# A mixture-of-experts transformer block: the first eight experts' results added to rows in DRAM by DMAs, the others scattered by matmuls as before, and activations turned in 32x32 blocks on VectorE

## The chip, the cores and the metric

The kernel runs on one core of one Trainium2 chip. The metric is the time of one execution on the device in microseconds (us); the median of three runs stands for the kernel. The profile is of one further execution of the same program. The engines are called by their short names: PE multiplies matrices (PEld is its loading of the stationary operand), DVE is VectorE, ACT is ScalarE, POOL is GpSimd, SP is SyncE, which here does nothing but issue DMAs.

## What is computed

One layer of a diffusion transformer over 512 tokens of width 1024: token mixing by latent attention and Fourier groups, then a mixture of experts that takes most of the time. Everything is float32. The part that matters here, cut from the reference:

```
logits = h @ w_router + b_router;  top_logit, top_idx = top_k(logits, 4)      # h: 512 x 1024, 32 experts
gates = softmax(top_logit)
per expert e, for the tokens that chose it:
    g = min(xb @ w_gate[e] + b_gate[e], 7);  u = clip(xb @ w_up[e] + b_up[e], -7, 7)
    y = (g * sigmoid(1.702 * g) * (u + 1)) @ w_down[e] + b_down[e]
    out[token] += gate * y
x + g2 * rms_norm(out, norm_ffn_post)
```

Each expert has three matrices of 1024 x 1024, 4.19 MB each. All 32 experts are read once, 402.7 MB together.

## The kernel before

The first quarter of the span is attention, Fourier mixing and the router. The rest is a chain of 32 **units**, one for each expert. A unit's **kind** says how many token slots it has: h 128, m 96, l 64, t 32. Units 0 and 1 are experts 0 and 1 (kind m). The other thirty experts are ranked by their number of tokens on the chip and fill fifteen **pairs**, one large unit and one small: units 2 and 3 are (m, t), 4 and 5 (m, l), 6 and 7 (m, l), 8 and 9 (h, t), and so on. In all there are 4 h, 13 m, 10 l and 5 t. An expert that has more tokens than its unit has slots is left to a loop after the end.

A unit has three **steps**, g, u and d, for its three matrices, written (4,g) and so on. `order` is written by hand: (0,g) (0,u) (1,g) (0,d) (1,u) (2,g) (1,d), and then, pair by pair, (3,g) (2,u) (3,u) (2,d) (3,d) (4,g) (5,g) (4,u) ... A step is eight chunks of 128 rows of its matrix. `step_mm` (L1538) multiplies one chunk: for an m unit twelve products of 32 stationary columns by 256 moving ones, in four column groups of PE that work side by side; for an l unit two products of 64 by 512; for a t unit four of 32 by 256; for an h unit six of 128 by 512 in the faster format float32r, high and low part of each operand apart. The profile counts a float32 product as two matmul instructions.

The weights come in **pieces** of two chunks (1 MB), issued by SP (`load_piece`, L965 to L978) into a ring of eleven slots. SP issues the next piece only when PE has done with the piece that held the slot. The queues of every engine run in the order in which the program is written; nothing is reordered.

Between its chunks a step does side work, one or two items a chunk (`side_step`): the tokens' rows are fetched from DRAM by an indirect DMA (`gather`, on POOL), turned by PE (`x_trans`), and after step u the activations are turned too. **`a_trans`** (L1441) does that in all kinds: PE transposes of 128 x 128 into PSUM (eight for h, six for m, four for l, two for t), copied to SBUF by ACT. `glu_g` and `glu_u` form the activations on DVE and ACT.

After step d the result must go to its tokens. **`y_out`** (L1475) copies it from PSUM, times the gate, as a high and a low part in float32r (ACT and DVE). `back` makes on DVE a table of ones that says which slot belongs to which token, and **`scatter`** (L1512) multiplies it with the result on PE: for each of four blocks of 128 tokens and two halves of 512 columns two products for an m or h unit and one for an l or t unit; DVE adds each sum to `acc`, four tiles of 128 x 1024 in SBUF. Unit 0 and unit 1 are scattered alone; from unit 2 on a pair is scattered together. The scatter of unit 0 has a third product that adds the gated `b_down` biases of all experts. After the last unit `acc` is normed and written out.

Of the kernel before, what the change touches and what calls it, by code (L numbers as in the profile page):

```python
# [36 lines left out]
D = 1024  # L37
# [125 lines left out]
def dit_block(ctx: ExitStack, tc: tile.TileContext, x, c, cctx, c_ctx, w_mod, b_mod, n_ap, n_ao, n_fp, n_fo,  # L163
# [6 lines left out]
    hx2_d = dr.tile([SEQ, D], F32, name="hx2_d")  # L170
    x1_d = dr.tile([SEQ, D], F32, name="x1_d")
    vec_d = dr.tile([4, D], F32, name="vec_d")

    NRING = 11
    NX = 5
# [1 line left out]
    WT = 1  # L177
    WN = {2: 4, 3: 4, 4: 4, 5: 4}
    NB, LA = 4, 3
    EARLY = (1, 2, 3)  # L180
    LATER = (0, 1, 1, 1, 1, 1, 1, 1)
    V = nc.vector
# [1068 lines left out]
        nc.gpsimd.memset(z.f, 0.0)  # L1251

    SLOTS = {"h": 128, "m": 128, "l": 64, "t": 32}

    def onehot_slots(kind, p_):
        n = SLOTS[kind]
# [32 lines left out]
    def gather(u, kind):  # L1289

        b = tbank()
        for t in range(4):
            mm(ps[:, b, 0:4], S1.r[:, t], R3[kind].r[:, t], start=t == 0, stop=t == 3)

        def fetch():
            cp(iv.f, ps[:, b, 0:4])
            stt(iv.f[:, 0:1], iv.f[:, 1:2], CRp("negT_" + ("h" if kind == "m" else kind)), iv.f[:, 0:1], op0=OP.mult, op1=OP.add)
            if u:
                tt(idxs.i[:, u:u + 1], iv.f[:, 0:1], CRp("addT_" + ("h" if kind == "m" else kind)), op=OP.add)
# [140 lines left out]

    def a_trans(kind):  # L1441
        a = glu_tiles(kind)[1]
        for half in range(2 if kind in "hm" else 1):
            b = tbank()
            n = min(4, WIDTH[kind] // 128 - 4 * half)
            for k in range(n):
                c = (4 * half + k) * 128
                tr(ps[:, b, k * 128:k * 128 + 128], a[:, c:c + 128])
            src = ps[:, b, 0:n * 128].rearrange("p (k n) -> p k n", k=n)
            c4 = slice(4 * half, 4 * half + 4)  # L1450
            if kind == "h":
                split_late(aTh.r[:, c4], aTl.r[:, c4], src)
            else:
                z = (aTm if kind == "m" else aTf.f)[:, 4 * half:4 * half + n]
                later(lambda src=src, z=z: act(z, src, AF.Copy), [z], [src], age=0)
            yield

    def glu_g(kind, b):
        t_, u_ = glu_tiles(kind)
# [8 lines left out]
    def glu_u(kind, b, wait=1):  # L1468
        t_, u_ = glu_tiles(kind)
        ts(u_, sums(kind, b), LIMIT, -LIMIT, op0=OP.min, op1=OP.max)  # L1470
        stt(u_, u_, 1.0, t_, op0=OP.add, op1=OP.mult)
        for _ in range(wait):
            yield

    def y_out(u, kind, b):  # L1475
        g = gcol.f[:, u:u + 1]
# [35 lines left out]
    def scatter(*us):  # L1512

        for t in range(4):
            for h in range(2):
                b = tbank()
                c, tk = slice(512 * h, 512 * h + 512), slice(128 * t, 128 * t + 128)
                terms = []
                for u in us:
                    if kinds[u] in "hm":  # L1520
                        rw = slice(0, 128 if kinds[u] == "h" else 96)
                        terms += [(ST["h"].r[rw, tk], z.r[rw, c]) for z in (yh, yl)]
                    else:
                        terms.append(small_term(kinds[u], tk, h))
                if us == (0,):
                    terms.append((gT.r[0:96, tk], bd.r[0:96, c]))
# [3 lines left out]
                if us == (0,):  # L1530
                    later(lambda z=z, b=b: cp(z, ps[:, b]), [z], [ps[:, b]], age=0)
                else:
                    later(lambda z=z, b=b: tt(z, z, ps[:, b], op=OP.add), [z], [z, ps[:, b]], age=0)
            yield

    MAT = {"g": 0, "u": 1}
# [1 line left out]
    def step_mm(kind, mat, b, k, w, hi, lo, sel, xs):  # L1538

        first = k == 0  # L1540
        if kind == "h":
# [6 lines left out]
            for st, mv, last in ((xh, hi, False), (xh, lo, False), (xl, hi, k == 7)):  # L1548
                for h in range(2):
                    mm(ps[:, b + h], st.r[:, k], mv.r[:, h * 512:h * 512 + 512], start=first, stop=last)  # L1550
                first = False
        elif kind == "m":
# [8 lines left out]
            both = ps[96:128, b].rearrange("p (r n) -> p r n", r=2)  # L1561
            if first:
                bias = biasP.b[0:96, MAT.get(mat, 0)]
                if mat != "d":
                    for p in range(3):
                        mm(out_(0, p, 2), sel.to_broadcast([96, 32]), bias[:, 0:512], start=True, stop=False)
                else:
                    sel = selb.b[0:96, NS + 2:NS + 3]
                mm(both, sel.to_broadcast([96, 32]), bias[:, None, 768:D].to_broadcast([96, 2, 256]), start=True,
                   stop=False)  # L1570
                if mat != "d":
                    for p in range(4):
                        q = unit(2, p)[1]
                        mm(out_(2, p), sel.to_broadcast([96, 32]), bias[:, q * 256:q * 256 + 256], start=True, stop=False)
            for r in range(3):
                for p in range(4):
                    g, q = unit(r, p)
                    n = 1
                    if mat != "d":
                        st = xs[:, k, 32 * g:32 * g + 32]  # L1580
                    else:
                        fq, c = k // 2, k % 2
                        st = xs[:, 2 * fq + c, 32 * g:32 * g + 32] if fq < 3 else xs[:, 2 * g + c, 96:128]
                        if first and p < 3 and r < 2:
                            if r:
                                continue
                            n = 2
                    mm(out_(r, p, n), st, w[:, q * 256:q * 256 + 256 * n],
                       start=first and mat == "d" and (p < 3 or r == 2), stop=k == 7 and r > 0)
        else:  # L1590
            v, n = (64, 512) if kind == "l" else (32, 256)
            a, c = k // (n // 128), k % (n // 128)
            st = xs[:, c, v * a:v * a + v]
            if first and mat != "d":
                for h in range(128 // v):
                    mm(ps[v * h:v * h + v, b, 0:n], sel.to_broadcast([96, v]),
                       biasP.b[0:96, MAT[mat], h * n:h * n + n], start=True, stop=False)
                first = False
            for h in range(128 // v):
                mm(ps[v * h:v * h + v, b, 0:n], st, w[:, h * n:h * n + n], start=first, stop=k == 7)  # L1600

    def sel_of(u):
        kind, e, r = units[u]
# [69 lines left out]
    for i, (u, m) in enumerate(order):  # L1673
        kind = kinds[u]
        if i:
# [2 lines left out]
            if was == "g":  # L1678
                add(glu_g(pk, pb), True)
            elif was == "u":  # L1680
                acted[pu] = add(chain(glu_u(pk, pb, {"h": 2, "m": 2, "l": 3, "t": 5}[kind]), a_trans(pk)), True)
            else:
                finish(summed)
                y_out(pu, pk, pb)
                if pu == 1:
                    summed = add(chain(chain_back(pu), scatter(pu)))
                elif pk in "lt":
                    summed = add(chain(chain_back(pu - 1), chain_back(pu), scatter(pu - 1, pu)))
        if i == 5:
            summed = add(chain(bdown(), chain_back(0), scatter(0)))  # L1690
        if i == 1:
            ready[1] = add(x_of(1))
        elif i == 2:
# [27 lines left out]
        elif i == 1:  # L1721
# [5 lines left out]
            aTm = alias(aTh, 6, 128)  # L1727
            yh, yl = R(D), R(D)
            acc = [W(D) for _ in range(4)]

            bdr = acc[3]
# [7 lines left out]
        elif i == 6:  # L1739
# [1 line left out]
                finish(side.pop(0))  # L1741
            settle()
            free(bd, g3, gT)
            aTf, u1l, yz = W(4, 128), W(512), R(D)

    while side:
        finish(side.pop(0))
# [136 lines left out]
```

## Time and profile before

| | |
|---|---|
| median of three runs | 1416.8 us (1412.1 to 1417.2) |
| the profiled execution's own time | 1413.2 us |
| its span, first to last instruction | 1411.4 us |
| PE busy | 1345.5 us, 95% of the span |
| DVE, ACT, POOL busy | 719.9, 409.3, 121.8 us |
| bytes moved by DMA | 468.9 MB, mean 332 GB/s |

The share of busy time of PE must be read with care: the ends of matmuls are modelled, and a busy engine may still be paced by something else. The rate of the DMAs in a stretch, and the time from one PE group's start to the next one's, say more. The expert part begins at about 338 us and its last product ends at about 1388 us.

### The profile page before, as it was taken

Reading aid. Unit: us, or ns where it says so; the run is one execution under the profiler, and the core shown is the slowest. Engines: PE = TensorE matmul, PEld = TensorE weight load, DVE = VectorE, ACT = ScalarE, POOL = GpSimd, SP = SyncE. Lnnn points to the kernel's source line nnn. Section 1 sums busy time; section 2 is a strip of 40 time slices with the busy share of each in tenths; the row PEclk is TensorE's granted clock in tenths of the full one; section 3 lists DMA queues with packets and bytes.
Section 4 is the critical chain, followed back from the end, with each engine's and each line's share of the span. In section 5 each row is a group of like instructions: output and inputs, shape, how many; then the busy total and the mean of one; then the engine's idle time right before and its main releaser. Section 6 shows DMA issues by size and latency. Waiting matters only on the chain. (4 is left out here: it accounts for less than half of the span.)

```text
span 1411.4 us, 30490 instructions
## 1 busy us (share of the span) xinstructions
PE 1345.5 (95%) x12966; PEld 798.2 (57%) x12967; DVE 719.9 (51%) x1329; ACT 409.3 (29%) x634; POOL 121.8 (9%) x90
## 2 busy tenths in 40 slices
PE   5998999998999999999999999999999999999993
PEld 3766887877554545466444454654544466444572
DVE  4676777755452424268423335762324287232575
ACT  5565455632110101035110103421111154010352
POOL 4355000013000000000000000000000000000002
PEclk8999999999998999999999999999999999999997
DMA  9865003667887999999999999999999999999993
GB/s 343 306 229 189 1 0 106 216 228 313 315 295 298 408 397 408 379 409 392 405 409 379 409 374 409 396 408 406 393 384 385 401 395 408 402 408 375 408 380 122
DMA packets 126496, 468.86 MB, mean 332 GB/s; under 512 B 10976, under 2 KB 12316, under 8 KB 126356
## 3 DMA queue, kind: packets, MB, share of 16 engines
q1 hardware_dynamic: 121540, 454.44, 83.2%
q0 software_dynamic: 4816, 12.43, 2.3%
q8 instruction: 103, 1.69, 0.5%
q14 instruction: 37, 0.30, 0.1%
HBM read 464.05 MB, written 6.31 MB: 333 GB/s over the span
## 5 line engine op out<-in xcount | busy, mean ns | idle before, releaser
L266 PE MATMUL ps<-s,s 128*32 128x256 f32 (+11 forms) x5364 | 892.4, 417 | 28.7 <-DMA s<-in_w_mod_dram 8.4
L266 PEld LDWEIGHTS ps<-s,s 128*128 128x128 f32 (+4 forms) x5033 | 510.8, 155 | 315.2 <-issue 182.2
L266 PE MATMUL ps<-s,a 128*32 128x256 f32 (+1 forms) x7026 | 412.7, 383 | 0.0
L266 PEld LDWEIGHTS ps<-s,a 128*32 128x32 f32 x7026 | 216.7, 110 | 158.5 <-issue 18.9
L274 ACT ACTIVATE s<-s 128x1024 fp32r<-128x1024 f32 (+8 forms) x196 | 175.9, 927 | 361.7 <-DVE s L283 308.4
L278 DVE TENSOR_TENSOR s<-s,s 128x1024 fp32r<-128x1024 f32 (+11 forms) x316 | 208.4, 686 | 32.3 <-ACT s L274 28.6
L274 ACT ACTIVATE s<-ps 128x512 fp32r<-128x512 f32 (+5 forms) x168 | 91.3, 553 | 246.0 <-PE ps L266 127.1
L278 DVE TENSOR_TENSOR s<-s,ps 128x512 f32<-128x512 f32 (+1 forms) x129 | 86.5, 682 | 82.1 <-PE ps L266 81.7
L285 DVE TENSOR_SCALAR s<-ps 128x768 f32<-128x768 f32 (+3 forms) x32 | 26.3, 823 | 185.1 <-PE ps L266 185.1
L270 PE MATMUL ps<-s,s 128*128 128x128 f32 x575 | 96.6, 288 | 15.3 <-DVE s L283 9.9
L1302 POOL DMA_INDIRECT s<-hx_d,s x31 | 32.4, 1045 | 893.3 <-PE ps L266 613.2
L270 PEld LDWEIGHTS ps<-s,s 128*128 128x128 f32 x575 | 66.4, 143 | 73.7 <-issue 45.8
L293 DVE COPY s<-ps 128x4 f32<-128x4 f32 (+5 forms) x66 | 23.7, 359 | 141.0 <-PE ps L266 117.0
L274 ACT ACTIVATE a<-ps 128x512 f32<-128x512 f32 (+1 forms) x48 | 25.9, 540 | 219.0 <-PE ps L270 219.0
L278 POOL TENSOR_TENSOR s<-s,s 128x1024 f32<-128x1024 f32 (+1 forms) x23 | 53.7, 2339 | 272.9 <-DVE s L278 211.4
L289 DVE SCALAR_TENSOR_TENSOR s<-ps,s,s 32x256 fp32r<-32x256 f32 (+5 forms) x64 | 46.2, 721 | 58.0 <-ACT s L274 52.0
L274 ACT ACTIVATE s<-ps,s 32x256 fp32r<-32x256 f32 (+7 forms) x68 | 44.8, 669 | 97.9 <-PE ps L266 90.5
L297 DVE TENSOR_TENSOR s<-ps,s 128x512 fp32r<-128x512 f32 (+1 forms) x92 | 60.6, 667 | 22.9 <-ACT s L274 22.8
L283 DVE TENSOR_SCALAR s<-ps 128x768 f32<-128x768 f32 (+4 forms) x33 | 26.5, 803 | 77.6 <-PE ps L266 77.5
L274 ACT ACTIVATE s<-s,s 128x1 f32<-128x1 f32 (+4 forms) x70 | 43.2, 644 | 13.8 <-DVE s L289 7.7
L297 DVE TENSOR_TENSOR s<-s,s 128x192 fp32r<-128x192 f32 (+5 forms) x32 | 36.0, 1144 | 8.5 <-ACT s L274 8.5
L289 DVE SCALAR_TENSOR_TENSOR s<-s,s,s 128x512 fp32r<-128x512 f32 (+5 forms) x48 | 36.8, 796 | 5.9 <-ACT s L274 4.6
(77 smaller groups left out, 289.4 us busy)
## 6 DMA issues: line engine op xcount, KB each, us to landing
s<-in_w_gate_dram SPq DMA_DIRECT2D x128, 1024.0 KB, 10.9
s<-in_w_up_dram SPq DMA_DIRECT2D x128, 1024.0 KB, 10.8
s<-in_w_down_dram SPq DMA_DIRECT2D x128, 1024.0 KB, 7.9
s<-in_w_mod_dram SPq DMA_DIRECT2D x32, 512.0 KB, 4.6
s<-in_w_mod_dram SPq DMA_DIRECT2D x8, 1024.0 KB, 16.3
s<-in_x_dram SPq DMA_DIRECT2D x8, 512.0 KB, 8.3
s<-in_w_out_dram SPq DMA_DIRECT2D x8, 512.0 KB, 5.1
s<-in_w_in_dram SPq DMA_DIRECT2D x1, 2560.0 KB
```

The costliest lines, as they stand in the source:

```text
L266: pin(nc.tensor.matmul(o, a, b, start=start, stop=stop))
L270: pin(nc.tensor.transpose(o, i, ident))
L274: return nc.scalar.activation(o, i, f, **kw)
L278: return eng.tensor_tensor(o, a, b, op=op)
L283: eng.tensor_scalar(o, a, s1, s2, op0=op0)
L285: eng.tensor_scalar(o, a, s1, s2, op0=op0, op1=op1)
L289: V.scalar_tensor_tensor(o, a, s, b, op0=op0, op1=op1)
L293: eng.tensor_copy(o, i)
L297: later(lambda: eng.tensor_tensor(lo, src, hi, op=OP.subtract), [lo], [src, hi])
L1302: nc.gpsimd.indirect_dma_start(out=xg[kind], out_offset=None, in_=src, in_offset=bass.IndirectOffsetOnAxis(ap=idxs.i[:, u:u + 1], axis=0), ...
```

## The change

It has two parts.

**Adding in DRAM.** For units 0 to 7 (`NADD = 8`) there is no `y_out`, no `back` and no `scatter`. `y_rows` copies the result times its gate from PSUM to one SBUF tile (`yd`, or `yd2` for l and t) in plain float32, and `y_send` has POOL issue one indirect DMA that adds its rows to those of `acc_d` in DRAM; unused slots point outside and are skipped. Before the first of them `first_rows` forms the bias product, copies it to `acc` on ACT and writes the four tiles to `acc_d` (2 MB). After unit 7's rows are sent, POOL issues four DMAs that read `acc_d` back into `acc` (2 MB), and units 8 to 31 are scattered by PE as before.

**Turning on VectorE.** For m, l and t units steps g and u are laid out anew: the stationary operand is 32 tokens, and the four column groups of PE take four interleaved sets of columns, each of eight runs of 32 columns of the chunk (`cols`). An m unit still has twelve products a chunk, a t unit four; an l unit has eight of 32 by 256 in place of two of 64 by 512. With that layout `a_trans` is one DVE transpose of 32 x 32 blocks for each 32 tokens, from SBUF to SBUF (three for m, two for l, one for t), without PE, PSUM or ACT. Units of kind h are unchanged.

```diff
@@ a_trans @@
+        if kind == "h":
...
+            return
+        for s in range(ROWS[kind] // 32):
+            o = (aTm if kind == "m" else aTf.f)[:, :, 32 * s:32 * s + 32]
+            i_ = a[:, 256 * s:256 * s + 256].rearrange("p (b r) -> p b r", r=32)
+            guard([o], [i_])
+            V.transpose(o, i_)
+        yield
@@ new @@
+    def y_rows(u, kind, b):
+        g = gcol.f[:, u:u + 1]
...
+            for s in range(3):
+                rw, cl = slice(32 * s, 32 * s + 32), slice(256 * s, 256 * s + 256)
+                cp(yd[rw, c3], y[96:128, cl])
+            act(yd[0:96, 0:768], y[0:96], AF.Copy, scale=g[0:96])
+            ts(yd[0:96, c3], yd[0:96, c3], g[0:96], None, op0=OP.mult)
+        else:
+            act(yd2[:, 0:WIDTH[kind]], ps[:, b, 0:WIDTH[kind]], AF.Copy, scale=g)
+    def y_send(u):
...
+        nc.gpsimd.indirect_dma_start(out=acc_d if nt == 1 else acc_d.rearrange("t (c n) -> (t c) n", c=nt),
+                                     out_offset=bass.IndirectOffsetOnAxis(ap=idxs.i[rw, u:u + 1], axis=0), in_=src,
+                                     in_offset=None, bounds_check=nt * SEQ - 1, oob_is_err=False, compute_op=OP.add)
+    def first_rows():
+        for t in range(4):
+            for h in range(2):
+                b = tbank()
+                c, tk = slice(512 * h, 512 * h + 512), slice(128 * t, 128 * t + 128)
+                mm(ps[:, b], gT.r[0:96, tk], bd.r[0:96, c], start=True, stop=True)
+                act(acc[t].f[:, c], ps[:, b], AF.Copy)
+            nc.gpsimd.dma_start(acc_d[128 * t:128 * t + 128], acc[t].f)
+            yield
+        y_send(0)
@@ step_mm, steps g and u of m, l and t @@
+            def cols(z, q):
+                return z.rearrange("p (b q r) -> p q b r", q=4, r=32)[:, q]
...
+            for s in range(n):
+                for q in range(4):
+                    mm(tile_(q, s), x_cols(32 * s), cols(w, q), start=False,
+                       stop=k == 7 and (s % 2 == 1 or s + 1 == n))
@@ after a step d @@
-                y_out(pu, pk, pb)
-                if pu == 1:
-                    summed = add(chain(chain_back(pu), scatter(pu)))
-                elif pk in "lt":
+                if pu < NADD:
+                    y_rows(pu, pk, pb)
+                    if pu:
+                        y_send(pu)
+                    if pu + 1 == NADD:
+                        for t in range(4):
+                            nc.gpsimd.dma_start(acc[t].f, acc_d[128 * t:128 * t + 128])
+                else:
+                    y_out(pu, pk, pb)
+                if pk in "lt" and pu >= NADD:
                     summed = add(chain(chain_back(pu - 1), chain_back(pu), scatter(pu - 1, pu)))
         if i == 5:
-            summed = add(chain(bdown(), chain_back(0), scatter(0)))
+            summed = add(chain(bdown(), first_rows()))
```

The first place where the order on an engine changes is PE's step (3,g), a t unit, in which unit 1 was scattered. Before, its rows begin like this (`s_3463` is the t unit's x, `s_3015` and `s_3016` are the high and low part of unit 1's result, `s_2719` the table of ones):

```order
L266 MATMUL ps<-s_2537,s_3463 32x256 x8
L266 MATMUL ps<-s_3015,s_2719 128x512
L266 MATMUL ps<-s_3016,s_2719 128x512
L266 MATMUL ps<-s_3015,s_2719 128x512
L266 MATMUL ps<-s_3016,s_2719 128x512
L266 MATMUL ps<-s_2545,s_3463 32x256 x4
```

With the change the same step on PE reads as follows (`s_3459` is the t unit's x); it goes from its bias products straight through its chunks:

```order
L268 LDWEIGHTS s_2598
L268 MATMUL ps<-s_1973,s_2598 32x256
L268 MATMUL ps<-s_2538,s_3459 32x256 x8
L268 MATMUL ps<-s_2546,s_3459 32x256 x8
L268 MATMUL ps<-s_2554,s_3459 32x256 x8
L268 MATMUL ps<-s_2562,s_3459 32x256 x8
```

No product of the scatter is left in that step. The second place is POOL's queue from the fetch of unit 4 on, which before held fetches alone (`hx_d` are the tokens' rows, `s_2733` and `s_2734` the buffers of large and of small units):

```order
L1302 DMA s_2733<-hx_d,s_2729 128x1024
L1302 DMA s_2734<-hx_d,s_2729 128x512
```

With the change the same stretch of POOL's queue holds the writes of `acc_d` and the adding DMAs between the fetches (`a_3018` is `yd`, `a_3731` is `yd2`):

```order
L1305 DMA s_2734<-hx_d,s_2730 128x1024
L1514 DMA acc_d<-s_3019 128x1024
L1514 DMA acc_d<-s_3020 128x1024
L1514 DMA acc_d<-s_3021 128x1024
L1514 DMA acc_d<-s_3022 128x1024
L1502 DMA acc_d<-a_3018,s_2730 512x1024
L1305 DMA s_2735<-hx_d,s_2730 128x512
L1502 DMA acc_d<-a_3018,s_2730 512x1024
```

The first adding DMA follows the four writes, and the fetch of unit 5 stands behind it in the queue.

## Rows read from the trace of the kernel before

**Rows 1.** The page: busy time of PE, then the DMAs' rate in 40 slices.

```profile
PE 1345.5 (95%) x12966; PEld 798.2 (57%) x12967; DVE 719.9 (51%) x1329; ACT 409.3 (29%) x634; POOL 121.8 (9%) x90
...
GB/s 343 306 229 189 1 0 106 216 228 313 315 295 298 408 397 408 379 409 392 405 409 379 409 374 409 396 408 406 393 384 385 401 395 408 402 408 375 408 380 122
```

**Rows 2.** Windows: from:to, us, busy (count) by engine, PEclk, DMA share, GB/s.

```profile
410.00:460.00 50.00, 47.13 (x603) 25.61 (x605) 18.75 (x36) 3.59 (x7) 1.00 (x1) 0.86 0.74 274
460.00:1372.00 912.00, 902.82 (x9204) 473.65 (x9193) 412.45 (x749) 204.95 (x291) 27.29 (x26) 1.00 1.01 398
480.00:490.00 10.00, 8.09 (x110) 4.56 (x114) 5.57 (x18) 1.86 (x4) 1.00 (x1) 1.00 1.03 408
```

**Rows 3.** Waits: of SP's queue in the whole span, of PE from 460 to 1380.

```profile
SPq L978 <- PE ps L266: 728.5, 323, 21.3
...
PE ps L266 <- DVE s L278: 6.8, 8, 1.8
```

**Rows 4.** Timeline of PE in step (1,g): start, us, what, count.

```profile
366.50 0.66 PE L270 MATMUL ps<-s,s 128*128 128x128 f32 x4
367.08 1.50 PE L266 MATMUL ps<-s,s 128*32 128x256 f32 x24
368.52 0.44 PE L270 MATMUL ps<-s,s 128*128 128x128 f32 x2
368.89 6.06 PE L266 MATMUL ps<-s,s 128*32 128x256 f32 x100
```

**Rows 5.** Timeline of PE: scatter of unit 0 in (2,g), then step (3,g).

```profile
406.55 1.68 PE L266 MATMUL ps<-s,s 96*128 96x512 f32 x6
...
430.30 1.16 PE L266 MATMUL ps<-s,s 96*32 96x256 bf16 x20
434.33 13.73 PE L266 MATMUL ps<-s,s 96*128 96x512 f32 x72 [2.87 <-DVE s L283]
447.88 4.49 PE L266 MATMUL ps<-s,a 128*32 128x256 f32 x80
```

**Rows 6.** Timeline of PE: one of four groups, scatters of (2,3) and (4,5).

```profile
487.73 2.23 PE L266 MATMUL ps<-s,s 96*128 96x512 f32 x6 [0.41 <-DVE s L283]
...
556.16 1.67 PE L266 MATMUL ps<-s,s 96*128 96x512 f32 x6
```

**Rows 7.** The page: software queue (packets, MB, share), DMA issues.

```profile
q0 software_dynamic: 4816, 12.43, 2.3%
...
x_d<-s POOLq DMA_DIRECT2D x4, 512.0 KB, 3.7
hx_d<-s POOLq DMA_DIRECT2D x4, 512.0 KB, 6.1
...
s<-hx_d,s POOLq DMA_INDIRECT x31, 6.8
```

**Rows 8.** Groups by shape, DVE, 440 to 1380 us.

```profile
L283 DVE TENSOR_SCALAR s<-ps 128x768 f32<-128x768 f32 x10 | 9.6, 958 | 20.7 <-PE ps L266 20.7
L289 DVE SCALAR_TENSOR_TENSOR s<-s,s 128x256 f32<-128x256 f32 x5 | 2.1, 424 | 0.2
```

**Rows 9.** Timeline of PE: value products in attention; half of an l unit's step u.

```profile
210.50 1.67 PE L266 MATMUL ps<-s,s 128*128 128x256 f32 x12
...
521.41 3.84 PE L266 MATMUL ps<-s,s 96*64 96x512 bf16 x18
```

**Rows 10.** The end: SP's load after the weights, a window, ACT's copy of unit 31.

```profile
1372.91 0.35 SPq L1754 DMA_DIRECT2D s<-vec_d  x1
...
1370.00:1375.00 5.00, 5.00 (x24) 3.93 (x23) 4.97 (x7) 4.40 (x6) 0.00 (x0) 1.00 0.92 353
...
1383.38 1.92 ACT L274 ACTIVATE s<-ps,s 32x256 fp32r<-32x256 f32 x4 [0.99 <-PE ps L266]
```

**Rows 11.** Windows around the scatter of unit 1, columns as in the second group.

```profile
430.00:440.00 10.00, 7.13 (x56) 3.35 (x44) 4.86 (x8) 2.05 (x4) 0.14 (x1) 0.68 0.75 301
440.00:450.00 10.00, 10.00 (x92) 5.02 (x92) 3.72 (x7) 0.42 (x1) 0.00 (x0) 0.64 0.52 182
```

More of the change, by code (lines that the diff above doesn't have):

```diff
@@ L172, in dit_block @@
     vec_d = dr.tile([4, D], F32, name="vec_d")
+    acc_d = dr.tile([SEQ, D], F32, name="acc_d")
     NRING = 11
@@ L179, in dit_block @@
     NB, LA = 4, 3
+    NADD = 8
     EARLY = (1, 2, 3)
@@ L1297, in fetch @@
             stt(iv.f[:, 0:1], iv.f[:, 1:2], CRp("negT_" + ("h" if kind == "m" else kind)), iv.f[:, 0:1], op0=OP.mult, op1=OP.add)
+            tt(idxs.i[:, u:u + 1], iv.f[:, 0:1], CRp("addT_" + ("h" if kind == "m" else kind)), op=OP.add)
             if u:
-                tt(idxs.i[:, u:u + 1], iv.f[:, 0:1], CRp("addT_" + ("h" if kind == "m" else kind)), op=OP.add)
                 nt = 128 // SLOTS[kind]
@@ L1442, in a_trans @@
         a = glu_tiles(kind)[1]
[L1443 to L1451, printed above, removed]
-                split_late(aTh.r[:, c4], aTl.r[:, c4], src)
[L1453 to L1456, printed above, removed]
+        if kind == "h":
+            for half in range(2):
+                b = tbank()
+                for k in range(4):
+                    c = (4 * half + k) * 128
+                    tr(ps[:, b, k * 128:k * 128 + 128], a[:, c:c + 128])
+                src = ps[:, b].rearrange("p (k n) -> p k n", k=4)
+                c4 = slice(4 * half, 4 * half + 4)
+                split_late(aTh.r[:, c4], aTl.r[:, c4], src)
+                yield
[6 more added lines that the diff above has]
+        yield
     def glu_g(kind, b):
@@ L1473, in glu_u @@
             yield
+    def y_rows(u, kind, b):
+        g = gcol.f[:, u:u + 1]
+        if kind == "h":
+            act(yd, flat2(b, D), AF.Copy, scale=g)
+        elif kind == "m":
+            y, c3 = flat2(b, 768), slice(768, D)
+            for s in range(3):
[6 more added lines that the diff above has]
+    def y_send(u):
+        kind = kinds[u]
+        nt, rw = 128 // SLOTS[kind], slice(0, 96 if kind == "m" else 128)
+        src = yd[rw] if kind in "hm" else yd2[:, 0:WIDTH[kind]]
+        guard([], [src, idxs.i[:, u:u + 1]])
+        nc.gpsimd.indirect_dma_start(out=acc_d if nt == 1 else acc_d.rearrange("t (c n) -> (t c) n", c=nt),
[4 more added lines that the diff above has]
+            for h in range(2):
+                b = tbank()
+                c, tk = slice(512 * h, 512 * h + 512), slice(128 * t, 128 * t + 128)
+                mm(ps[:, b], gT.r[0:96, tk], bd.r[0:96, c], start=True, stop=True)
+                act(acc[t].f[:, c], ps[:, b], AF.Copy)
+            nc.gpsimd.dma_start(acc_d[128 * t:128 * t + 128], acc[t].f)
+            yield
+        y_send(0)
     def y_out(u, kind, b):
@@ L1529, in scatter @@
                 z = acc[t].f[:, c]
[L1530 to L1533, printed above, removed]
+                later(lambda z=z, b=b: tt(z, z, ps[:, b], op=OP.add), [z], [z, ps[:, b]], age=0)
             yield
@@ L1551, in step_mm, with x_cols, tile_ @@
                 first = False
+        elif mat != "d":
+            n = ROWS[kind] // 32
+            def x_cols(o):
+                m, v = {"m": (8, 0), "l": (4, 64), "t": (2, 32)}[kind]
+                return xs[:, k % m, v * (k // m) + o:v * (k // m) + o + 32]
+            def cols(z, q):
+                return z.rearrange("p (b q r) -> p q b r", q=4, r=32)[:, q]
+            def tile_(q, s, n=1):
+                return ps[32 * q:32 * q + 32, b + s // 2, 256 * (s % 2):256 * (s % 2) + 256 * n]
+            if first:
+                for s in range(0, n, 2):
+                    m = min(2, n - s)
+                    for q in range(4):
+                        z = cols(biasP.b[0:96, MAT[mat]], q)
+                        o = tile_(q, s, m)
+                        if m == 2:
+                            o = o.rearrange("p (m b r) -> p m b r", m=2, r=32)
+                            z = z[:, None].to_broadcast([96, 2, 8, 32])
+                        mm(o, sel.to_broadcast([96, 32]), z, start=True, stop=False)
+            for s in range(n):
+                for q in range(4):
+                    mm(tile_(q, s), x_cols(32 * s), cols(w, q), start=False,
+                       stop=k == 7 and (s % 2 == 1 or s + 1 == n))
         elif kind == "m":
@@ L1558, in out_ @@
                 return ps[32 * p:32 * p + 32, b + r // 2, 256 * (r % 2):256 * (r % 2) + 256 * n]
-            both = ps[96:128, b].rearrange("p (r n) -> p r n", r=2)
             if first:
[L1563 to L1574, printed above, removed]
+                both = ps[96:128, b].rearrange("p (r n) -> p r n", r=2)
+                zero = selb.b[0:96, NS + 2:NS + 3].to_broadcast([96, 32])
+                mm(both, zero, biasP.b[0:96, 0][:, None, 768:D].to_broadcast([96, 2, 256]), start=True, stop=False)
             for r in range(3):
@@ L1578, in step_mm @@
                     n = 1
[L1579 to L1589, printed above, removed]
+                    if first and p < 3 and r < 2:
+                        if r:
+                            continue
+                        n = 2
+                    mm(out_(r, p, n), xs[:, k, 32 * g:32 * g + 32], w[:, q * 256:q * 256 + 256 * n],
+                       start=first and (p < 3 or r == 2), stop=k == 7 and r > 0)
         else:
             v, n = (64, 512) if kind == "l" else (32, 256)
[L1592 to L1598, printed above, removed]
             for h in range(128 // v):
-                mm(ps[v * h:v * h + v, b, 0:n], st, w[:, h * n:h * n + n], start=first, stop=k == 7)
+                mm(ps[v * h:v * h + v, b, 0:n], xs[:, k, 0:v], w[:, h * n:h * n + n], start=first, stop=k == 7)
     def sel_of(u):
@@ L1726, in dit_block @@
             aTh, aTl = R(8, 128), R(8, 128)
-            aTm = alias(aTh, 6, 128)
+            aTm = alias(aTh, 8, 96)
             yh, yl = R(D), R(D)
+            yd = alias(yh, D)
             acc = [W(D) for _ in range(4)]
@@ L1743, in dit_block @@
             free(bd, g3, gT)
-            aTf, u1l, yz = W(4, 128), W(512), R(D)
+            aTf, u1l, yz = W(8, 64), W(512), R(D)
+            yd2 = alias(yz, 512)
     while side:
```

5 lines of the change are left out of this document (2 added, 3 removed).

## The prediction

> **What bounds the kernel now.** I read the page first: PE is busy 95% of the span, and from slice 14 to slice 39 the DMAs move 374 to 409 GB/s [rows 1]. Both look full, so the question is which of them paces the other. The windows tell: where the DMAs are undisturbed they move 408 GB/s, also while POOL fetches rows; but from 460 to 1372 us they average 398, and from 410 to 460 only 274 [rows 2]. The list of waits says why. SP waits 728.5 us in all for PE to give a ring slot back, while in the expert part PE's longest entry is 6.8 us in total for DVE, and no DMA stands in its list at all [rows 3]. So **PE sets the pace**, by a small margin: the weights could come only some percent faster. The kernel has two limits close together, and a change must be counted against both.
>
> **PE's account.** Turning goes off PE. In an m unit four transposes stand from 366.50 to 367.08 us and two from 368.52 to 368.89 [rows 4]: 0.58 + 0.37 = 0.95 us. An l unit has four (0.58), a t unit two (0.37). For 13 m, 10 l and 5 t that is 12.4 + 5.8 + 1.9 = 20.0 us.
>
> The scatters of units 0 to 7 go too. Unit 0's are four groups of 1.68 us [rows 5], of which a third, the bias product, stays: 4 x 1.68 x 2/3 = 4.5 us. Unit 1's lie in step (3,g), which takes from 430.30 to 447.88 us, 17.6 us [rows 5]. Its own work is 64 instructions; 80 of that size take 4.49 us, so 3.6 us are its own and 14.0 us go: PE first stands 2.87 us for DVE's table of ones, and then runs at half its clock, 1.2 GHz, for a while (mean 0.68 and 0.64 in two windows [rows 11]). Units 2 and 3 have four groups of 2.23 us, 8.9 us; units 4 and 5 four of 1.67, 6.7 us, and 6 and 7 the same [rows 6]. Together 40.8 us.
>
> The new layout of steps g and u costs PE nothing if a strided moving operand is read as fast as a plain one. For an l unit a chunk becomes sixteen instructions of 4.49/80 = 0.056 us, 0.90 us; now eighteen instructions (four chunks and the bias) take 3.84 us, 0.9 a chunk [rows 9]. The count for m and t stays.
>
> So PE alone would end 20.0 + 40.8 = 60.8 us sooner. Against the profiled execution's own 1413.2 us (span 1411.4) that is **1352 us**, if the weights were always there.
>
> **The DMAs' account.** They are not. From 410 us on the stream carries 50 x 274 + 912 x 398 kB = 376.7 MB up to 1372 us [rows 2]. At 408 GB/s that takes 923.2 of the 962 us: 38.8 us of slack, no more, whatever PE saves. I start at 410 because there the ring is full and PE is at the first scatter; before it PE loses only unit 0's transposes, 1 us.
>
> The change also adds bytes, on the same DMAs. `acc_d` is written once and read once: 2 x 2.10 MB. The adds carry the same rows as the fetches. POOL's queue moved 12.43 MB, of which the eight DMAs of x_d and hx_d are 4.19 [rows 7]; the rest over 31 fetches is 0.266 MB each, so eight adds hold 2.13 MB. No row shows an adding DMA. Below I price it like a fetch (factor 1); above like four fetches. I take 2, since it must read the old row as well as the new one. That gives 4.19 + 4.25 = 8.44 MB or 20.7 us; 15.5 us at factor 1, 31.1 at 4. The Trainium skill (Collectives: The Full Stack, The bandwidth ceiling) says that an add in the DMA path needs two source reads for one write; by that the price is again twice a copy's. No run here shows it.
>
> The stream thus saves 38.8 - 20.7 = **18.1 us** (7.7 to 23.3).
>
> **The end and the beginning.** The last weights land at about 1373.7 us (353 GB/s in 1370 to 1375, with vec_d's 0.5 MB in it), and ACT copies the last unit's result at 1383.4 [rows 10]. PE lags 9.7 us behind the stream now, since it is the slower one; paced by the stream it lags one piece of a t unit, 0.9 us. That is 0 to 8.8 us; I take 6, because in the (m, l) pairs PE stays about as slow as the stream. With 1 us from the start: 1413.2 - 18.1 - 6 - 1 = **1388 us**. Since 1388 lies above 1352, the DMAs are the bound and two thirds of PE's saving turns into waits for weights.
>
> **What hides the rest.** DVE's transposes take about 0.42 us per 256 columns (its nearest rows, 424 and 958 ns for 256 and 768 [rows 8]); three and the two operations before them are 3.2 us, behind the small unit's step u of 7 us (l) or 3.6 us (t). With twice the price it is 4.5 us, which only the single (m, t) pair would feel. If that cover were gone, 28 units would pay up to 3 us each. The adds bring one new wait: `yd` is filled again for unit 1 when unit 0's add has landed. That add waits for the four writes of `acc_d` (3.7 to 6.1 us to land [rows 7]) and itself needs about 6.8. DVE and ACT may stand some 5 us there, behind them unit 2's activations; PE has steps (3,g) and (2,u), about 14 us, before it asks for those. On POOL the fetch of unit 5 stands behind that add and is needed two steps later still. Both cost nothing. What becomes late in place of PE is the weights: PE should wait for them first in (2,d) to (5,u), when the ring has run empty.
>
> **The rivals.** *Strided reads* (slower). If PE reads runs of 32 columns 128 apart more slowly, steps g and u pay: 16 chunks x (13 x 1.34 + 10 x 0.90 + 5 x 0.45) = 459 us of work. From 8% PE is the bound again (1352 + 37 = 1389), from 13% nothing is gained, at 20% it is 1352 + 92 = 1444 us. The nearest row speaks against it: the value products of attention read two runs of 128 columns 256 apart, twelve in 1.67 us, 0.14 us for 256 columns with the loading [rows 9], near one column a cycle; but their runs are longer. Chance 0.1.
>
> *Dear adds.* The gain is gone when the added traffic takes 46 us, that is, when an add costs 6.9 times a fetch. At 8 it is 1413.2 - 38.8 + 52 - 7 = 1419 us. Against it: a fetch by the same queue leaves the total at 408 GB/s [rows 2]. Chance 0.08.
>
> *A falling clock.* PE that waits for weights may drop to 1.2 GHz, as it did after the 2.87 us wait. There the clock was halved for (0.32 + 0.36) x 2 x 10 = 13.6 us [rows 11], 6.8 us of work. In pairs 2/3 to 8/9 PE has some 7 us of idle time a pair, which one fall uses up; two a pair in three pairs would make it 1388 + 3 x 6 = 1406 us. Against it: between 480 and 490 PE stood idle for 1.9 us and the clock stayed at 1.00 [rows 2], and waits for a piece in an l or t step are shorter than that. The Trainium skill (TensorE: Matmul & The Clock Gate, HAM oscillation) warns of this: a loop whose waits for data are longer than its products falls back to the low clock again and again. By that rule it would be the 1406. Chance 0.1.
>
> *No effect on the stream.* If the dips in the rate were not PE's doing, the slack of 38.8 us could not be used and the added bytes would count in full: 1413.2 + 20.7 - 7 = 1427 us. SP's 728.5 us of waits for PE [rows 3] speak against it. Chance 0.05.
>
> **How the numbers follow.** The forecast has 0.62 and a range of its own, 1380 (23.3, 8.8 and 1 us) to 1404 (7.7, 0 and 1 us). A measurement of this kernel can tell about 0.5% from no change, here 7 us. The remaining 0.05 is for an end nearer to PE's 1352. Faster takes the forecast, the falling clock for the most part, and half of the dear adds: 0.77. Slower takes the strided reads from 15% on, the dear adds above 8 and the stream without effect: 0.13. Between them 0.10. For 8 in 10 I go from 1373, somewhat below the forecast's own low end, to 1409, above the falling clock; strided reads and the stream without effect are left out. The median of three runs stood 3.6 us above the profiled execution before, so I give 1389.
>
> **What would show it.** Right: from 410 us to the end the DMAs at 405 to 411 GB/s with no dips; PE waiting for in_w_gate, in_w_up or in_w_down some 30 us in all, most of it between 470 and 680; step (3,g) in about 4 us at full clock; no transposes by PE in m, l and t units; the last copy of ACT about 3 us after the last weights. Adds of about 7 us to landing. Wrong: chunks of an m unit's step g slower than 1.34 us (strided reads), dips below 400 GB/s while SP waits for no slot (dear adds), PEclk below 1.00 in several windows (the clock), or DVE in the list of PE's waits with more than 10 us.

## The result

The changed kernel takes 1398.9 us (median of four runs, 1397.7 to 1401.2) against 1414.5 us of the kernel before on the same chip: a ratio of 0.9896, 95% interval 0.9875 to 0.9917. It is faster by 15.6 us; the forecast was 1389, some 25 us faster. The profiled execution took 1397.7 us, its span 1396.0. Measured once more on another chip, the ratio was 0.9929 (0.9911 to 0.9947), 10.0 us. So the gain is clear of noise, and 10 to 16 us.

The page of the changed kernel: the busy time of PE, its granted clock in 40 slices, the DMAs' rate, the software queue [rows 1, 7].

```profile
PE 1294.3 (93%) x14694; PEld 813.9 (58%) x14695; DVE 708.4 (51%) x1343; ACT 385.5 (28%) x581; POOL 139.6 (10%) x106
...
PEclk8999999999999999989999999999999999999996
...
GB/s 342 314 238 185 1 1 107 217 226 319 311 364 397 397 408 391 408 394 409 405 407 407 407 407 406 408 401 406 406 405 402 407 408 401 396 408 404 409 374 120
...
q0 software_dynamic: 6960, 18.81, 3.9%
```

PE is busy 51 us less, but the end came only 15 us sooner. The deep dips of before (374 to 385 GB/s) are gone but for the last two slices. The windows by stage show what is left of them (columns as in [rows 2]):

```profile
410.00:460.00 50.00, 48.94 (x832) 28.58 (x824) 18.51 (x56) 5.21 (x9) 7.74 (x7) 1.00 1.03 396
460.00:1372.00 912.00, 868.05 (x10780) 500.31 (x10777) 410.81 (x751) 185.43 (x246) 36.50 (x34) 0.99 1.02 401
...
460.00:595.00 135.00, 120.30 (x1800) 62.20 (x1796) 31.62 (x79) 8.83 (x14) 9.36 (x8) 0.96 1.03 400
595.00:668.00 73.00, 57.39 (x370) 38.76 (x372) 42.76 (x62) 29.96 (x33) 7.29 (x7) 0.88 1.03 403
668.00:842.00 174.00, 173.56 (x2567) 95.46 (x2559) 62.64 (x132) 16.46 (x28) 4.99 (x5) 1.00 1.02 407
842.00:924.00 82.00, 77.70 (x635) 49.16 (x629) 59.67 (x104) 34.01 (x41) 3.44 (x3) 1.00 1.02 407
```

From 410 to 668 us PE is idle for 31 us of 258 and the DMA engines are full (share 1.03). From 668 to 842, in (m, l) pairs, PE is busy all the time again. From 842 to 924, around the h pair (16, 17), it stands idle for 4 us. PE's list of waits from 410 to 668 us:

```profile
PE ps L268 <- ACT s L276: 10.1, 3, 4.6
PE ps L268 <- DMA s<-in_w_gate_dram: 9.9, 6, 4.3
PE ps L268 <- DMA s<-in_w_up_dram: 7.2, 10, 1.7
PE ps L268 <- DVE s L280: 2.0, 3, 1.2
PE ps L268 <- DMA s<-in_w_down_dram: 1.9, 3, 0.9
```

19.0 us are waits for weights, where before had none. The longest wait for ACT is one too, at second hand: ACT splits the weights of the h unit 8 into a high and a low part, and it got them late. Another of 2.5 us is of the same kind. PE's timeline, three rows, and ACT's, one:

```profile
422.83 4.08 PE L268 MATMUL ps<-s,s 96*32 96x256 bf16 x76
...
464.34 13.20 PE L268 MATMUL ps<-s,a 128*32 128x256 f32 x192 [4.29 <-DMA s<-in_w_gate_dram]
...
624.09 16.12 PE L268 MATMUL ps<-s,s 128*128 128x512 f32 x80 [4.56 <-ACT s L276]
```

```profile
622.98 2.00 ACT L276 ACTIVATE s<-s 128x1024 fp32r<-128x1024 f32 x2 [8.34 <-DMA s<-in_w_up_dram]
```

The first of these rows is step (3,g) [rows 5]: it began at 422.8 and (2,u) followed at 426.4, 3.6 us after, at full clock.

The next table holds the time (us, from the span's start) at which a step's first bias product starts, read from PE's records in each profile, and the start of ACT's last copy [rows 10]. Between (8,g) and (10,g) lies an h pair, as between (16,g) and (18,g); between (10,g) and (16,g) lie three (m, l) pairs.

| kernel | (3,g) | (8,g) | (10,g) | (16,g) | (18,g) | (30,g) | last copy | span |
|---|---|---|---|---|---|---|---|---|
| before | 430.3 | 617.8 | 676.4 | 877.4 | 936.0 | 1329.1 | 1383.4 | 1411.4 |
| whole change | 422.8 | 595.3 | 668.5 | 862.5 | 924.2 | 1309.7 | 1366.8 | 1396.0 |
| turning alone | 426.7 | 605.1 | 664.1 | 858.0 | 917.1 | 1301.0 | 1358.1 | 1386.1 |
| adding alone | 427.4 | 598.2 | 671.1 | 872.2 | 930.8 | 1323.9 | 1378.2 | 1406.3 |
| units 0 and 1 added | 425.9 | 600.8 | 663.2 | 857.2 | 919.8 | 1304.5 | 1361.8 | 1390.6 |
| nothing sent | 421.7 | 582.6 | 647.8 | 841.8 | 903.7 | 1289.7 | 1346.4 | 1374.4 |
| half weights | 422.2 | 571.4 | 624.0 | 818.0 | 877.1 | 1259.0 | 1313.7 | 1343.0 |
| turning, scatter later | 425.2 | 597.6 | 656.7 | 850.7 | 909.7 | 1293.8 | 1350.2 | 1378.3 |

The whole change is 22.5 us ahead of the kernel before at (8,g) and 7.9 at (10,g): pair (8, 9) takes 73.2 instead of 58.6 us. Three (m, l) pairs then win 7 us, the h pair (16, 17) gives 3 back, and so on to 16.6 us at the last copy. (The stages before (0,u) move the start by up to 5 us from one profile to another, so single differences of a few us between columns of different kernels prove little.)

### The profile page after: what moved, and what is told of

Read it like the earlier page. It is cut to its first block, busy times and chain, and to the rows that moved or that the text cites. A ratio compares the mean times of both kernels' runs of the same rounds, so it can differ in the third digit from the quotient of the medians.

```text
span 1396.0 us, 33930 instructions
## 1 busy us (share of the span) xinstructions
PE 1294.3 (93%) x14694; PEld 813.9 (58%) x14695; DVE 708.4 (51%) x1343; ACT 385.5 (28%) x581; POOL 139.6 (10%) x106
## 3 DMA queue, kind: packets, MB, share of 16 engines
q0 software_dynamic: 6960, 18.81, 3.9%
## 5 line engine op out<-in xcount | busy, mean ns | idle before, releaser
L268 PE MATMUL ps<-s,s 128*32 128x256 f32 (+12 forms) x7220 | 855.3, 386 | 50.3 <-ACT s L276 17.4
L268 PEld LDWEIGHTS ps<-s,s 128*32 128x32 f32 (+3 forms) x6849 | 527.9, 139 | 310.2 <-issue 93.1
L268 PE MATMUL ps<-s,a 128*32 128x256 f32 (+1 forms) x7026 | 413.2, 386 | 10.4 <-DMA s<-in_w_gate_dram 6.0
L280 DVE TENSOR_TENSOR s<-s,s 128x1024 fp32r<-128x1024 f32 (+10 forms) x317 | 208.9, 683 | 69.5 <-ACT s L276 57.1
L280 DVE TENSOR_TENSOR s<-s,ps 128x512 f32<-128x512 f32 (+1 forms) x97 | 64.8, 680 | 60.0 <-PE ps L268 59.6
L272 PE MATMUL ps<-s,s 128*128 128x128 f32 (+1 forms) x447 | 74.7, 290 | 17.9 <-DVE s L285 10.7
L272 PEld LDWEIGHTS ps<-s,s 128*128 128x128 f32 (+1 forms) x447 | 53.5, 146 | 53.5 <-issue 17.1
L295 DVE COPY s<-ps 128x4 f32<-128x4 f32 (+7 forms) x53 | 16.0, 303 | 118.9 <-PE ps L268 99.9
L276 ACT ACTIVATE s<-ps,s 32x256 fp32r<-32x256 f32 (+8 forms) x55 | 35.6, 661 | 73.9 <-PE ps L268 69.2
L276 ACT ACTIVATE a<-ps 128x512 f32<-128x512 f32 x22 | 13.1, 596 | 146.2 <-PE ps L272 146.1
L291 DVE SCALAR_TENSOR_TENSOR s<-s,s 128x1 f32<-128x1 f32 (+3 forms) x71 | 37.5, 529 | 2.4
```

Of the source, the lines that this page charges most:

```text
L268: pin(nc.tensor.matmul(o, a, b, start=start, stop=stop))
L272: pin(nc.tensor.transpose(o, i, ident))
L276: return nc.scalar.activation(o, i, f, **kw)
L280: return eng.tensor_tensor(o, a, b, op=op)
L291: V.scalar_tensor_tensor(o, a, s, b, op0=op0, op1=op1)
L295: eng.tensor_copy(o, i)
```

## The experiments

All ratios are to the kernel before, on the chip of the run.

| kernel | us (median) | ratio, 95% interval |
|---|---|---|
| turning alone | 1388.2 | 0.9840 (0.9817 to 0.9863) |
| adding alone | 1408.1 | 0.9981 (0.9972 to 0.9990) |
| units 0 and 1 added | 1391.6 | 0.9859 (0.9841 to 0.9877) |
| nothing sent | 1376.9 | 0.9762 (0.9745 to 0.9778) |
| plain writes for adds | 1392.6; again 1391.3 | 0.9874 (0.9852 to 0.9897); 0.9865 (0.9847 to 0.9883) |
| half weights | 1345.8 | 0.9544 (0.9520 to 0.9567) |
| turning, scatter of unit 1 later | 1383.9; again 1381.5 | 0.9807 (0.9787 to 0.9827); 0.9797 (0.9780 to 0.9813) |
| before, scatter of unit 1 later | 1404.7 | 0.9953 (0.9935 to 0.9971) |
| whole change again | 1399.6 | 0.9929 (0.9911 to 0.9947) |
| no round trip of acc_d | 1389.3 | 0.9855 (0.9838 to 0.9873) |

**Turning alone.** `NADD = 0`; `y_out` and `scatter` for all units as before.

```diff
-    NADD = 8
+    NADD = 0
...
-            summed = add(chain(bdown(), first_rows()))
+            summed = add(chain(bdown(), chain_back(0), scatter(0)))
```

> The turning on VectorE and its layout alone; all units are scattered by PE as before, acc_d isn't written, added to or read. Theory (the two limits alternate: the weight stream holds units 4 to 9 and the h pairs, PE holds the m-l pairs): unit 1's scatter costs its 17 us again, but no added bytes follow, so step (10,g) comes about as early as with the whole change (8 us sooner than before) and the m-l pairs take 63.8 us instead of 66.2: about 1398 us (1394 to 1403), as fast as the whole change. Rival (the gain is a sum over PE's saved work, scaled down): turning is 20 of 60.8 us, so a third of the 15.6 us: about 1409.

1388.2 us: half the change is better than the whole, by some 10 us (8 to 13 by the ratios, which stand for two chips), and both expectations are missed. PE's list of waits holds no weights (9.9 and 5.0 us for two lines of DVE at the most), but for the last two chunks PE's loading of the stationary operand does wait for them, as shown below. The (m, l) pairs take 63.6 to 66.6 us where before took 65.9 to 68.9, 2.35 us less each. My theory was right that the bounds alternate, but wrong in taking (10,g) to come no sooner: without the added bytes it came 4 us sooner than with them, and the rest up to the last copy took 4 us less.

**Adding alone.** `a_trans`, `step_mm` and their tiles as before, `NADD = 8`.

> The adding in DRAM alone; PE transposes and the plain layout of steps g and u as before. Theory: step (10,g) comes some 7 us sooner than before, as with the whole change, since the stream sets it; from there on nothing is won, the m-l pairs take 66.2 us and the h pairs 58.6 again: about 1407 us (1403 to 1411). Rival (sum over PE's saved work): 40.8 of 60.8 us, two thirds of the 15.6 us: about 1404, and not told apart by the time; by the pairs' times it is.

1408.1 us, a gain of 0.2%, as the theory had it. In the table the 5 us that it is ahead at (10,g) stay as they are to the last copy.

**Units 0 and 1 added.** `NADD = 2`.

> NADD = 2: units 0 and 1 added in DRAM, units 2 to 7 scattered by PE again (22 us of PE work back, six adds fewer, acc_d still written and read once). Theory: between (4,g) and (10,g) PE waits for weights anyway, so the 22 us fall into its waits, and the stream has six adds of about 1.4 us less, 8 us: step (10,g) comes up to 8 us sooner than with the whole change, and the end with it: about 1392 us (1387 to 1397), with PE waiting for weights less. Rival (PE paces): slower than the whole change by up to 22 us, 1405 or more. Rival (the falls of PE's clock are what is missing, adds are cheap): same as the whole change or slower.

1391.6 us, as the theory had it: 22 us of PE's scatters are back, the kernel is faster, and PE waits for weights for 6.2 us from 410 to 668 us instead of 19.0. But it is no faster than turning alone.

**Nothing sent.** Without `y_send` and all eight DMAs of `acc_d`.

> The whole change without its DMAs to and from acc_d: y_rows forms the rows, but nothing is written, added or read back, so the results of units 0 to 7 are missing from the output. Theory: the stream carries 8.3 MB less, 22 us by the time the packets took; (10,g) comes 15 to 22 us sooner than with the whole change, and the end some 12 to 18 us: about 1384 us (1378 to 1390). Rival (clock falls and waits between engines hold it, the DMAs' bytes hardly matter): 1394 to 1399. Rival (adds cost far more than twice a copy): below 1378.

1376.9 us, below the theory's range and just inside that of the rival of dear adds. The bytes cost the change about 22 us (1398.9 and 1399.6 less 1376.9; 19 to 24 by the ratios, since the chips differ). That is the whole time that their packets took (the software queue's share falls from 3.9% to 2.4% of the span, 21 us), and more than the theory's 12 to 18.

**No round trip** (neither the four writes of `acc_d` nor the four DMAs that read it back) and **plain writes** (the rows written and not added) split those 22 us. The whole change ran beside the first and beside the second run of plain writes on one chip; it came out at 0.9929, a little outside what I expected of it.

> The whole change without writing acc_d and reading it back (2 x 2.1 MB); the eight adds stay, but what they add is lost to the output. Theory (the stream is short of every byte): 4.19 MB at 408 GB/s, 10 us, so 8 to 10 us faster than the whole change; with the adds gone too (nothing sent) it was some 19 to 22 us, so the adds keep 9 to 12. Rival (the adds are what costs, the plain copies hide): 0 to 4 us faster.

> The whole change with its eight adding DMAs writing rows plainly instead of adding them (so a token's row in acc_d holds the last result written and not the sum); the writes of acc_d and its reading back stay. Theory (an add takes about twice a copy of the same rows on the DMAs, 1.4 us against 0.7): eight times 0.7, up to 6 us less: about 1394 us (1391 to 1397 where the whole change takes 1399). Rival (adds take several times a copy): 1385 or less. Rival (adds take no more than a copy): as the whole change, 1398 to 1400.

> Plain writes in place of the adds, once more beside the whole change on one chip, since the intervals of the first measurement overlapped (output: a token's row holds the last result and not the sum). Theory (an add holds the DMAs twice as long as a plain write): 3 to 6 us faster than the whole change. Rival (no dearer): within 1 us of it.

> The whole change once more, on the chip of the next three runs: a ratio of 0.9885 to 0.992 to the kernel before. No theory hangs on it but as their measure.

```diff
-                                     in_offset=None, bounds_check=nt * SEQ - 1, oob_is_err=False, compute_op=OP.add)
+                                     in_offset=None, bounds_check=nt * SEQ - 1, oob_is_err=False)
```

Writing and reading `acc_d` costs 10.3 us (1399.6 less 1389.3), what 4.19 MB take at 408 GB/s. The eight adds cost the other 12.4 us (1389.3 less 1376.9, on two chips; 13 by the ratios). Plain writes of the same rows would save 8.3 of them (1399.6 less 1391.3), more than the 3 to 6 that I expected. Windows of the kernel with plain writes and of the whole change beside it:

```profile
410.00:460.00 50.00, 49.32 (x844) 29.02 (x840) 18.50 (x56) 5.48 (x9) 5.94 (x6) 1.00 1.03 407
460.00:595.00 135.00, 118.94 (x1781) 61.15 (x1774) 34.16 (x86) 11.76 (x17) 7.01 (x8) 1.00 1.03 408
```

```profile
410.00:460.00 50.00, 48.81 (x832) 28.56 (x820) 18.51 (x56) 5.57 (x10) 7.15 (x6) 1.00 1.02 395
460.00:595.00 135.00, 120.76 (x1814) 61.82 (x1816) 31.62 (x79) 9.04 (x14) 10.24 (x8) 0.96 1.03 401
```

The queue moves the same 18.81 MB in both, the DMA engines are full in both, but while rows are added they move 395 and 401 GB/s instead of 407 and 408. In the pages the software queue's packets take 3.5% of the engines' time with plain writes and 3.9% with adds: 0.4% of 1390 us is 5.6 us more for the same bytes.

**Half weights.** Only the first chunk of each piece is loaded.

```diff
-        return where[u, m, k // 2].f[:, k % 2]
+        return where[u, m, k // 2].f[:, 0]
...
-        nc.sync.dma_start(slot.f, src.rearrange("e (k p) f -> p (e k) f", p=128)[:, 2 * h:2 * h + 2])
+        nc.sync.dma_start(slot.f[:, 0:1], src.rearrange("e (k p) f -> p (e k) f", p=128)[:, 2 * h:2 * h + 1])
```

> The whole change with half of each weight piece loaded (both chunks of a piece are multiplied with the first one's rows, so the experts' results are of other weights); PE's, DVE's and ACT's work is the same. The stream can't be the limit. Theory: PE's own pace, with no waits for weights: m-l pairs 63.8 us, h pairs 58.6 again in place of 61 to 73, no clock below 1.00 after 460 us: about 1352 us (1345 to 1360). Rival (PE loses the time to the clock or to waits for DVE and ACT whatever the weights do): 1375 or more.

1345.8 us. As the theory had it, with the weights always there PE is busy nearly all the time and its clock stays up; the windows of this run:

```profile
460.00:595.00 135.00, 134.87 (x1920) 77.18 (x1913) 52.47 (x103) 26.59 (x32) 14.55 (x13) 1.00 0.82 268
...
842.00:924.00 82.00, 79.65 (x958) 48.49 (x956) 44.29 (x74) 19.83 (x26) 1.99 (x2) 1.00 0.66 214
```

So the loads hold the whole change back by some 53 us. In the table its (m, l) pairs from (10,g) to (16,g) take 194.0 us, and with half the weights 194.0 too; its h pairs take 73.2 and 61.7, against 52.6 and 59.0. **The limits alternate**: in (m, l) pairs PE is the slower one (63.6 us and more, the 25.17 MB of weights need 61.7 at 408 GB/s), in h pairs (59.0 with half the weights) and in units 4 to 9 the stream is.

**Scatter of unit 1 one step later**, once in the kernel of turning alone, once in the kernel before:

```diff
+    def pause(n):
+        for _ in range(n):
+            yield
...
-                    summed = add(chain(chain_back(pu), scatter(pu)))
+                    summed = add(chain(chain_back(pu), pause(8), scatter(pu)))
```

> The turning alone, and unit 1's scatter by PE one step later: in (2,u) instead of (3,g), so that DVE's table of ones is ready when PE comes to it. No DMA to or from acc_d. Theory: PE's wait of 2.9 us and the half clock that follows go, 4 to 7 us, and the stream fills 410 to 460 us at 380 GB/s or more instead of 315: about 1382 us (1378 to 1386), faster than the whole change by over 1 per cent. Rival (the stall was hidden, since the stream limits the rest): as turning alone, 1387 to 1390. Rival (the later scatter delays unit 2's activations): slower than turning alone.

> The kernel before with unit 1's scatter one step later, nothing else. Theory: PE sets the pace there, so the whole stall is won: step (3,g) 3.6 us, the scatter about 7 us in (2,u), together some 10.5 instead of 17.3 us: 6 to 7 us faster than before (ratio 0.995 to 0.996), more than the adding in DRAM alone gave (0.998). Rival (weights set the pace already): no change, 0.999 to 1.001.

> Turning alone with unit 1's scatter one step later, beside the whole change on one chip: a ratio of 0.979 to 0.983 to the kernel before, 10 to 15 us faster than the whole change. Rival (the difference came from the chips): within 5 us of the whole change.

Before with this one edit takes 1404.7 us, 6.6 us less, more than adding in DRAM won alone. With turning it takes 1383.9 and 1381.5 us: the fastest complete version here. The second run is 18 us faster than the whole change beside it, more than the 10 to 15 expected. The DMAs move 372 GB/s from 410 to 460 us, a little less than the theory's 380, against 315 in turning alone. PE in turning alone, then in this kernel:

```profile
426.68 1.16 PE L268 MATMUL ps<-s,s 96*32 96x256 bf16 x20
430.69 10.98 PE L268 MATMUL ps<-s,s 96*128 96x512 f32 x72 [2.86 <-DVE s L285]
```

```profile
425.16 4.08 PE L268 MATMUL ps<-s,s 96*32 96x256 bf16 x76
429.06 2.77 PE L268 MATMUL ps<-s,a 128*32 128x256 f32 x48
431.76 1.19 PE L268 MATMUL ps<-s,s 96*128 96x512 f32 x4
432.88 1.50 PE L268 MATMUL ps<-s,a 128*32 128x256 f32 x24
```

In the first, PE waits 2.86 us for DVE's table. In the second the table is ready, each of four groups of the scatter takes 1.1 us, and (3,g) and (2,u) together take 19.3 us instead of 25.2.

## Why the prediction was half right

*PE paces the kernel before, by a small margin*: right. One stall of PE removed there gave its 6.6 us.

*Turning, 20.0 us*: right in kind, too low. It gave 23.4 us alone (1411.5 to 1388.2). PE's own saving is larger still, some 28 us as an estimate, since two h pairs of that kernel already wait for weights: they take 61.2 us from (24,g) to (26,g) and 57.1 us from (30,g) to the last copy, with half the weights 59.0 and 54.7. An (m, l) pair lost 2.35 us where I had counted 0.95 + 0.58; the l unit's step u alone, in which the m unit's activations are turned, went from 8.46 to 7.15 us, 1.31 instead of 0.95. DVE's transposes cost what I took, and they stand nowhere in PE's list of waits (groups by shape):

```profile
L1461 DVE STREAM_TRANSPOSE a<-s 128x256 f32<-128x256 f32 x32 | 11.7, 416 | 0.3
L1461 DVE STREAM_TRANSPOSE s<-s 128x256 f32<-128x256 f32 x25 | 9.9, 428 | 0.5
```

*Strided operands cost nothing*: right; an l unit's step g takes 7.13 us (7.20 before), an m unit's step u 10.69 (10.80).

*The scatters, 40.8 us*: PE lost them, and (3,g) took the 3.6 us that I gave it. But what they were worth in time is 11.3 us (1388.2 less 1376.9, on one chip), since between (4,g) and (10,g) the weights took over.

*PE alone 1352 us*: 1345.8 with half the weights, as near as the low count of the turning lets it be.

*Added bytes, 20.7 us*: about 22 us measured. The round trip was 10.3 as forecast, the adds 12.4 instead of 10.4. The dearer bytes were right: I had taken a factor of 2, and in the packets' time it is 2. By the pages the software queue's share is 3.2% without the round trip and 2.4% with nothing sent, so the eight adds took 11.4 us of packets' time, and plain writes 5.6 us less. The Trainium skill (Collectives: The Full Stack, The bandwidth ceiling) gives two source reads for an added chunk of a collective; these packets' times agree. In the time of the kernel, plain writes would have cost 4.1 of the 12.4 us, a factor of 3, but each ratio is uncertain by 2.5 us, so 3 can't be told from 2. The queue moved 6.38 MB more, of which `acc_d` is 4.19.

*The stream saves 18.1 us*: **this step failed**. It is right for the mean rate of the DMAs, which falls at about 1354 us instead of 1373.7, 19.7 us sooner:

```profile
1340.00:1354.00 14.00, 13.04 (x108) 8.07 (x107) 8.64 (x10) 5.88 (x7) 0.00 (x0) 1.00 1.03 409
1354.00:1371.00 17.00, 15.64 (x114) 10.53 (x114) 10.86 (x16) 7.71 (x11) 0.00 (x0) 1.00 0.57 220
```

But I had treated the 16 DMA engines as one pipe, whose last bytes land when its full rate ends. The weights did not all land by then. Each load has sixteen landing records in the trace, and in the changed kernel the last three of them come late. For the last piece of weights (us; the lag is from the last part to ACT's last copy):

| kernel | 13th of 16 parts | last part | last copy | lag |
|---|---|---|---|---|
| before | 1374.6 | 1376.1 | 1383.4 | 7.3 |
| whole change | 1356.4 | 1365.6 | 1366.8 | 1.2 |
| turning alone | 1349.1 | 1356.9 | 1358.1 | 1.2 |
| adding alone | 1369.1 | 1370.4 | 1378.2 | 7.8 |
| nothing sent | 1337.9 | 1345.2 | 1346.4 | 1.2 |
| half weights | 1297.5 | 1297.5 | 1313.7 | 16.2 |

The thirteenth part came some 18 us sooner than before, the last one only 10.5, inside the range that I gave (7.7 to 23.3) but for a reason that it did not hold. The engines wait for the last part: ACT for pieces whose last parts landed at 1347.8 and 1355.5 us, and PE, before the last two chunks, for the one whose last part landed at 1365.6 (its loading of the stationary operand, PEld, stands still until then). The first three rows are of the whole change; the fourth is the same place in turning alone:

```profile
1347.97 1.06 ACT L276 ACTIVATE s<-s 128x1024 fp32r<-128x1024 f32 x1 [8.81 <-DMA s<-in_w_down_dram]
1355.56 1.06 ACT L276 ACTIVATE s<-s 128x1024 fp32r<-128x1024 f32 x1 [0.45 <-DMA s<-in_w_down_dram]
1365.63 0.59 PEld L268 LDWEIGHTS ps<-s,s 128*32 128x32 f32 x16 [0.44 <-DMA s<-in_w_down_dram]
...
1356.97 0.59 PEld L268 LDWEIGHTS ps<-s,s 128*32 128x32 f32 x16 [0.62 <-DMA s<-in_w_down_dram]
```

*The end, 6 us*: right, and partly by luck. ACT's last copy:

```profile
1366.77 1.92 ACT L276 ACTIVATE s<-ps,s 32x256 fp32r<-32x256 f32 x4 [1.16 <-PE ps L268]
```

It starts 1.2 us after the last weights, so at the end PE is indeed paced by the stream, as I had said (0.9 us). The lag shrank by 6.1 us, but from 7.3 and not from 9.7: the last weights of the kernel before landed at 1376.1 us, not at the 1373.7 that I had read from the rate. From the copy to the end it is 29.2 us (28.0 before). The sum is thus 10.5 + 6.1 - 1.2 = 15.4 us, the difference of the spans, where I had 18.1 + 6 + 1 = 25.1; the 1 us for the start can't be told from the 5 us by which starts vary.

The late parts are not the whole reason. With half the weights the stretch from (30,g) to the last copy takes 54.7 us, here 57.1, so at the end alone at most 2.4 us were to be won by earlier weights. The rest lies further ahead, and there a sum over the whole leaves something out: I asked which limit is the larger in total, and let it hold everywhere. But in the (m, l) pairs PE paces: its waits from 1181 to 1345 us are 0.7 us in all, none for weights. What those stages could win was PE's own saving, 2.35 us a pair; then an h pair waits for weights again. How much of that waiting an even landing of the sixteen parts would have removed, no run shows.

*Waits for weights of 30 us between 470 and 680*: 19.0 at first hand from 410 to 668 and, through ACT, 7.0 of the 10.1 (the waits of 4.6 and 2.5 us).

*The rivals*. The dear adds came nowhere near the 6.9 at which the gain is gone. The falling clock is there: 0.96 and 0.88 from 460 to 668 us, where PE waits for weights, and 1.00 with half the weights. In the Trainium skill (TensorE: Matmul & The Clock Gate, HAM oscillation) waits for data bring such falls again and again; here they ended when PE had work again, at 668. I find no price for them: the DMAs were full all that time, and with plain writes, where the clock is 1.00 from 460 to 595 us, PE's busy time is about the same (118.9 and 120.8 us). But no run takes the falls away and leaves the waits, so it stays open.

## What to carry to other kernels

Two limits that lie close change places along a kernel. Work out which holds in each stage, with a buffer that carries over no more than its depth (here 11.5 MB, 28 us of the stream), and not which is larger in total. Ask of a stream's end when its last transfer has landed in full, not when its mean rate falls: here nine us lay between thirteen of sixteen parts and the last. Where the stream is as full as here, moving work from an engine into DMAs is paid at the stream's full price; if an engine stalls because a table is late, move the consumer by one step first.

## What was not expected of the hardware

While rows are added in DRAM, the DMAs, as full as before (shares of 1.02 and 1.03), move fewer counted bytes: 395 and 401 GB/s, where plain writes of the same rows leave 407 and 408. No row tells whether an add also reads the old row, uncounted.

And where the stream runs full for long, the parts of a load drift apart. In the last piece of weights the sixteen landing records lie 1.6 to 2.5 us apart in the three kernels without turning (before, adding alone, before with the later scatter) and 0.7 us with half the weights, but 10.2 to 10.9 us in all ten other profiles. The adds are not the cause, since turning alone has 10.7 us. There the spread grows along the kernel, from 3.3 us at 560 to 11 at 1120, and then stays. So the rate trails off at the end: in the whole change the DMAs still moved 66 GB/s from 1365 to 1371 us. The records do not name the engines, and why three parts fall behind stays open.

```profile
1365.00:1371.00 6.00, 5.70 (x49) 3.46 (x39) 3.39 (x8) 2.46 (x6) 0.00 (x0) 1.00 0.16 66
```
